# Projection tiles in pairs by seven block products in place of eight, in a five-branch mixer kernel

## The chip, the cores and the metric

The kernel runs on one core of one Trainium2 chip. The metric is the device time of one execution in microseconds (us). The core has five engines that run side by side, each working off its own list of instructions in order: PE (TensorE: matmuls), DVE (VectorE), ACT (ScalarE), POOL (GpSimd) and SP (SyncE, which here only issues DMA transfers). PEld is the loading of PE's stationary operand.

## The reference, cut to what matters

One layer of a decoder: 1024 tokens, width 1024, all in float32.

```
proj = h @ w_in + b_in                      # h: 1024 x 1024 (normed x), 94 used column tiles of 128
A    gated delta rule, 4 heads              # q, k, v: 12 tiles
B    GLU -> causal conv of width 31 -> LayerNorm -> swish      # 8 tiles
C    sliding-window attention, 8 heads over 2 kv heads         # cq 4, ck 1, cv 1
D    width-4 conv -> gated linear recurrence (a scan)          # dx 4
E    attention into 256 memory tokens, 4 heads                 # eq 4; w_mem_kv
ys[n]      = branch[n] * silu(z[n])                            # z: 5 x 4 tiles
merged     = sum_n sigmoid(gate[n]) * (ys[n] @ w_br[n])        # gate: 5 x 8 tiles
out        = x + rmsnorm(merged @ w_out)
```

So most of the matrix work is `h @ w_in`: 94 tiles, each 1024 (contraction) x 128 (columns) against 1024 tokens. Each branch product `ys[n] @ w_br[n]` contracts over 512.

## The kernel before

Float32 precision is had by splitting every operand into a high and a low part (`F32R` tiles): `mm3` issues three matmuls for one product of a 128 x 128 weight block with 128 x 512 tokens (high·high, high·low, low·high). The transposed, normed input is held for nearly the whole run as 8 tiles `hTh[k]` (high) and 8 tiles `hTl[k]` (low), 128 x 1024 each.

A projection tile is one *unit*: `wload` loads 512 KB of weights into `raw`, ACT copies it to `wh` (L222), POOL computes the rest `wl` (L223); `project` runs 2 token halves x 8 contraction steps x 3 = 48 matmuls into a PSUM tile `mm` of two banks (two such tiles take turns), and ACT or DVE evicts it. Eight contraction steps, k = 0 to 7, are two halves of four; the tokens are two halves `HL` and `HR` of 512. The list `units` sets the order: branch A's tiles, B's, the silu gates `az`, `eq`, then for each branch n `m_units(n)`: two gate tiles, then one branch unit `br` (48 matmuls from the branch's halves `yh`, `yl`, for two column tiles), and so on, four times; the gate (`sg`, L1004) multiplies the product on DVE (L1029) and POOL adds it to `merged` (L1032). `z_units` multiplies a finished branch by its silu (L972, POOL L955) and splits it into `yh`, `yl` (L958, L959).

The branches' own work runs in the *background*: generators (`gdn_all`, `conv_b`, `attn_e`, `lru`, `attn_c`) that are advanced by `tick()`, which `project` calls after every second contraction step, that is 8 times a tile. `start_bg` gives each a rate (steps per tick): conv_b 1.1, attn_e 1.0, lru 0.6, attn_c 1.0. `drain` runs a generator to its end at once. The program fixes dependences and priorities (`tc.high_priority` lifts an instruction above others); a scheduler turns them into one list per engine when the kernel is built, so at run time an engine that waits at the head of its list holds up everything behind it.

Names: `pc` is the convolution's accumulator in PSUM (L876, 120 steps on DVE), `u` its input, `rt`, `it`, `a2`, `th` belong to `lru`, `woh`/`wol` are the split `w_out`.

## Time and profile before

| | |
|---|---|
| time, median of 3 runs | 1665.55 us (1665.54 to 1666.98) |
| profiled execution: time / span of its instructions | 1666.35 us / 1664.6 us |
| PE, DVE, ACT, POOL busy share of the span | 97%, 51%, 39%, 36% |
| mean granted PE clock | 0.988 of full speed |
| DMA | 87.5 MB, mean 53 GB/s |

The span runs from the first to the last instruction of the profiled execution; its device time is 1.75 us longer. A busy share is an average over stages that are bound by different things. Matmuls overlap, so the sum of their durations is more than the time they take.

### The profile page before, as it was taken

Reading aid. Unit: us, or ns where it says so; the run is one execution under the profiler, and the core shown is the slowest. Engines: PE = TensorE matmul, PEld = TensorE weight load, DVE = VectorE, ACT = ScalarE, POOL = GpSimd, SP = SyncE. Lnnn points to the kernel's source line nnn. Section 1 sums busy time; section 2 is a strip of 40 time slices with the busy share of each in tenths; the row PEclk is TensorE's granted clock in tenths of the full one; section 3 lists DMA queues with packets and bytes.
Section 4 is the critical chain, followed back from the end, with each engine's and each line's share of the span. In section 5 each row is a group of like instructions: output and inputs, shape, how many; then the busy total and the mean of one; then the engine's idle time right before and its main releaser. Section 6 shows DMA issues by size and latency. Waiting matters only on the chain.

```text
span 1664.6 us, 19410 instructions
## 1 busy us (share of the span) xinstructions
PE 1613.9 (97%) x7846; PEld 1327.6 (80%) x7846; DVE 842.4 (51%) x1257; ACT 655.0 (39%) x1071; POOL 596.7 (36%) x315
## 2 busy tenths in 40 slices
PE   8989699999999998999999999999999999999998
PEld 7668588888888876888888877788888888888877
DVE  6678844376898886233564634211066664002712
ACT  6344123532421124435445276522266654212311
POOL 1354232422422237612345266554221222622021
PEclk9899899999999999999999999999999999999999
DMA  4112110110011110222011111112110101112322
GB/s 156 46 40 64 38 33 26 38 39 26 13 64 51 45 45 27 88 70 95 26 39 51 51 38 51 39 51 76 51 39 26 39 26 39 51 51 76 102 97 80
DMA packets 27129, 87.51 MB, mean 53 GB/s; under 512 B 5104, under 2 KB 6560, under 8 KB 26912
## 3 DMA queue, kind: packets, MB, share of 16 engines
q1 hardware_dynamic: 26896, 86.15, 15.9%
q8 instruction: 61, 1.00, 0.3%
q14 instruction: 28, 0.23, 0.0%
q10 hardware_dynamic: 144, 0.13, 0.0%
HBM read 82.06 MB, written 5.78 MB: 53 GB/s over the span
## 4 chain that ended last, share of the span: by engine, by line
PE 80%; DVE 14%; ACT 3%; POOL 2%; issue 1%; DMA 0%; DVEq 0%; ACTq 0%; POOLq 0%
PE mm L278 22%; PE mm L277 22%; PE mm L279 22%; DVE qk L484 2%; DVE lt L692 2%; DVE Ad L694 1%; PE pb L1451 1%; DVE v L484 1%; PE pb L722 1%; PE pa L722 1%; PE pa L1407 1%; DVE m L612 1%; PE pb L1439 1%; PE pa L664 1%; DVE p L1183 1%
## 5 line engine op out<-in xcount | busy, mean ns | idle before, releaser
L279 PE MATMUL mm<-hTh,wl 128*128 128x512 f32 x1472 | 591.4, 402 | 10.8 <-POOL wl L223 10.8
L277 PE MATMUL mm<-hTh,wh 128*128 128x512 f32 x1472 | 599.6, 407 | 0.0
L278 PE MATMUL mm<-hTl,wh 128*128 128x512 f32 x1472 | 594.1, 404 | 0.0
L223 POOL TENSOR_TENSOR wl<-raw,wh 128x1024 fp32r<-128x1024 f32 x113 | 276.4, 2446 | 638.5 <-ACT wh L222 638.1
L279 PEld LDWEIGHTS mm<-hTh,wl 128*128 128x128 f32 x1472 | 279.2, 190 | 69.6 <-POOL wl L223 11.9
L277 PEld LDWEIGHTS mm<-hTh,wh 128*128 128x128 f32 x1472 | 279.5, 190 | 58.7 <-issue 0.2
L278 PEld LDWEIGHTS mm<-hTl,wh 128*128 128x128 f32 x1472 | 279.5, 190 | 55.1 <-issue 3.1
L222 ACT ACTIVATE wh<-raw 128x1024 fp32r<-128x1024 f32 (+1 forms) x131 | 129.8, 998 | 387.1 <-issue 246.2
L876 DVE SCALAR_TENSOR_TENSOR pc<-u,sm,pc 128x1024 f32<-128x1024 f32 x120 | 154.7, 1289 | 3.8
L277 PE MATMUL mm<-yh,wh 128*128 128x512 f32 x320 | 127.8, 399 | 0.0
L278 PE MATMUL mm<-yl,wh 128*128 128x512 f32 x320 | 127.4, 398 | 0.0
L279 PE MATMUL mm<-yh,wl 128*128 128x512 f32 x320 | 126.8, 396 | 0.0
L972 DVE SCALAR_TENSOR_TENSOR sg<-mm,sm,sg 128x1024 f32<-128x1024 f32 x20 | 25.7, 1284 | 121.9 <-ACT sg L971 90.2
L1032 POOL TENSOR_TENSOR merged<-merged,sg 128x1024 f32<-128x1024 f32 x24 | 59.1, 2461 | 57.2 <-DVE sg L1029 35.9
L277 PEld LDWEIGHTS mm<-yh,wh 128*128 128x128 f32 x320 | 60.1, 188 | 13.0 <-DVE sgl L1029 0.2
L278 PEld LDWEIGHTS mm<-yl,wh 128*128 128x128 f32 x320 | 60.2, 188 | 12.5 <-issue 1.5
L279 PEld LDWEIGHTS mm<-yh,wl 128*128 128x128 f32 x320 | 60.1, 188 | 12.6
L1029 DVE TENSOR_TENSOR sg<-mm,sg 128x1024 f32<-128x1024 f32 x27 | 32.9, 1220 | 48.1 <-PE mm L279 30.3
L223 DVE TENSOR_TENSOR wol<-raw,woh 128x1024 fp32r<-128x1024 f32 x8 | 9.9, 1234 | 90.0 <-ACT woh L222 90.0
L1397 DVE TENSOR_TENSOR ql<-yC,qh 64x512 fp32r<-64x512 f32 x32 | 27.6, 863 | 54.1 <-ACT qh L1394 53.7
L1451 PEld LDWEIGHTS pb<-vt,pT 128*128 128x128 f32 x240 | 43.2, 190 | 9.2 <-ACT pT L1440 2.6
L1577 POOL TENSOR_TENSOR res<-res,xr 128x512 f32<-128x512 f32 x14 | 17.8, 1293 | 84.2 <-DVE res L1575 76.5
(428 smaller groups left out, 2441.3 us busy)
## 6 DMA issues: line engine op xcount, KB each, us to landing
raw<-in_w_t SPq DMA_DIRECT2D x94, 512.0 KB, 3.7
raw<-in_w_br SPq DMA_DIRECT2D x20, 512.0 KB, 3.6
xt<-in_x SPq DMA_DIRECT2D x8, 512.0 KB, 7.9
raw<-in_w_mem SPq DMA_DIRECT2D x8, 512.0 KB, 3.8
raw<-in_w_out SPq DMA_DIRECT2D x8, 512.0 KB, 3.8
xr<-in_x SPq DMA_DIRECT2D x8, 512.0 KB, 4.6
out_dram<-res SPq DMA_DIRECT2D x7, 512.0 KB, 2.9
d_rt<-d_rb SPq DMA_DIRECT2D x1, 1536.0 KB, 8.6
```

The source lines that it names most:

```text
L222: act.activation(hi, raw, AF.Copy)
L223: eng.tensor_tensor(out=lo, in0=raw, in1=f32(hi), op=ALU.subtract)
L277: pe.matmul(o, lh, rh, start=start, stop=False)
L278: pe.matmul(o, lh, rl, start=False, stop=False)
L279: pe.matmul(o, ll, rh, start=False, stop=stop)
L484: dve.scalar_tensor_tensor(out=acc, in0=xp[:, j:j + 1024], scalar=cw(j), in1=acc, op0=ALU.mult, op1=ALU.add)
L692: dve.tensor_tensor(out=t3, in0=V3[:, 0:r, j:j + 1].broadcast_to([P, r, n]), in1=A3[:, j:j + 1, j + 1:32].broadcast_to([P, r, n]), op=ALU. ...
L722: pe.matmul(ps[:, j * P:(j + 1) * P], lhs[:, j, :], rhs[:, j, :], start=True, stop=True)
L876: dve.scalar_tensor_tensor(out=acc, in0=u[:, j:j + 1024], scalar=w(j), in1=acc, op0=ALU.mult, op1=ALU.add)
L1029: dve.tensor_tensor(out=(merged[d] if first else sgs[d])[:, cl], in0=p2, in1=sgs[d][:, cl], op=ALU.mult)
L1032: (dve if last else pool).tensor_tensor(out=merged[d][:, cl], in0=merged[d][:, cl], in1=sgs[d][:, cl], op=ALU.add)
L1451: pe.matmul(po[:, i, g, :], pts[n, g][:, m, i * P:(i + 1) * P], vt[:, k0 // P + m, 64 * g:64 * g + 64], start=(m == 0), stop=(m == nk - 1))
```

## The change

Two 128-column tiles k0, k1 of `w_in` are taken as one 2 x 2 block product: the weights have blocks (tile k0 or k1) x (contraction half), the input has blocks (contraction half) x (token half). Seven products of sums of blocks, in place of eight products of blocks, give all four result blocks; each is 4 contraction steps x 3 = 12 matmuls of 512 tokens. The names in `prod(...)` are the input's block sums: `b11`, `b21`, `b22` are halves of `hTh`/`hTl`; `t1` to `t4` are differences, computed once by `blocks_h` (`t1` overwrites a quarter of `hTh`/`hTl` by `block_t1`). The sums of weight blocks are made per pair: four DVE additions (`preps`) and seven splits (`wblock`, ACT and POOL, 512 columns each). Products accumulate in PSUM banks X (two take turns), Y and Z (one each), and a bank is read by ACT (`keep`) or DVE (`plus`) between two products that accumulate in it.

The 20 tiles of A's q, k, v and B's inputs and 10 gate tiles stay as plain units. The other 64 tiles are 32 pairs. Their results, and the gated halves `yh`, `yl` of branches A, B, E and D, are stored to DRAM (`dram(key)`) and loaded again where they are used. All branch products come last (`run_branches`), with `attn_c` as background. Rates now: conv_b 1.1 (2.0 after the convolution), attn_e 1.1, lru 1.2, attn_c 1.0. The PSUM pool `mm` is closed while the pairs run.

```diff
-    def project(hi, lo):
+    def project(hi, lo, between=None):
...
+    def gated(n, zk, t, y, z_t):
+        while (zk, t) not in dr:
+            yield
+        zt, b = z_t(F32), bcol(zk, t)
+        sp.dma_start(zt, dr[zk, t])
+        yield from wait(3)
+        s = z_t(F32)
+        act.activation(s, zt, AF.Sigmoid, bias=b)
+        dve.scalar_tensor_tensor(out=zt, in0=zt, scalar=b, in1=s, op0=ALU.add, op1=ALU.mult)
+        pool.tensor_tensor(out=y, in0=y, in1=zt, op=ALU.mult)
+        yield from wait(2)
+        h, l = z_t(F32R), z_t(F32R)
+        act.activation(h, y, AF.Copy)
+        pool.tensor_tensor(out=l, in0=y, in1=f32(h), op=ALU.subtract)
+        sp.dma_start(dram(("yh", n, t)), f32(h))
+        sp.dma_start(dram(("yl", n, t)), f32(l))
+        yield from wait(2)
...
+    def wblock(x):
+        t = wp.tile([P, 2, 512], F32R, name=nm("wb"), tag=("raw", "wh", "wl")[wtag[0] % 3])
+        wtag[0] += 1
+        act.activation(t[:, 0, :], x, AF.Copy)
+        pool.tensor_tensor(out=t[:, 1, :], in0=x, in1=f32(t[:, 0, :]), op=ALU.subtract)
+        return t
...
+            def prod(o, hn, start):
+                w = blk()
+                for k in range(4):
+                    ks = slice(k * P, (k + 1) * P)
+                    mm3(o, w[:, 0, ks], w[:, 1, ks], *hb[hn, k], start and k == 0, k == 3, not start)
+                    if k % 2:
+                        tick()
+            u0, u1 = sg_t(), sg_t()
...
+            prod(X, "b11", True)
+            keep(u0[:, HL], X)
+            prod(Z, "t1", True)
+            keep(u1[:, HR], Z)
+            prod(X, "t2", False)
+            keep(u0[:, HR], X)
+            prod(Y, "b21", True)
+            plus(u0[:, HL], Y)
+            prod(X, "t3", False)
+            plus(u1[:, HR], X)
+            prod(Z, "b22", False)
+            plus(u0[:, HR], Z)
...
+            prod(X, "t4", False)
...
+            sp.dma_start(dram(k0), u0)
+            sp.dma_start(dram(k1), u1)
...
+        order = quad("az") + quad("bz") + quad("eq") + quad("ez") + quad("dx") + quad("dz")
+        tail = quad("cq") + [(("ck", 0), ("cv", 0))] + quad("cz")
+        pairs.extend(order + gp[:4] + tail + gp[4:])
...
+    def y_load(n):
+        for t in range(4):
+            for d, s in ((yh, "yh"), (yl, "yl")):
+                if n == 0:
+                    d[n, t] = pools["m"].tile([P, T], F32R, name=nm(s), tag=s, bufs=4)
+                else:
+                    d[n, t] = hp_.tile([P, T], F32R, name=nm(s), tag="hT")
+                sp.dma_start(f32(d[n, t]), dr[s, n, t])
...
+    def run_branches():
+        pools["pc"], st_["pc"] = open_pool("pc")
+        start("c", attn_c, 1.0)
+        order = [(n, dp) for n in (0, 1, 4, 3, 2) for dp in range(4)]
+        gl = [(n, 2 * dp + e) for n, dp in order for e in range(2)]
+        for g in gl[:3]:
+            gate_load(*g)
+        ng = 3
+        y_load(1)
+        w = wload(a["w_br"][0, 0], False)
```

**Where the rows move, PE.** Before, a tile's matmuls all use one weight tile (`wh`, `wl`) and the eight `hTh`, `hTl`; here the first six of 48.

```order
L277 MATMUL mm_3751<-hTh_101,wh_3682 128x512
L278 MATMUL mm_3751<-hTl_109,wh_3682 128x512
L279 MATMUL mm_3751<-hTh_101,wl_3683 128x512
L277 MATMUL mm_3751<-hTh_102,wh_3682 128x512
L278 MATMUL mm_3751<-hTl_110,wh_3682 128x512
L279 MATMUL mm_3751<-hTh_102,wl_3683 128x512
```

Now, the first product of the first pair (bank X, weight block `wb_3827`) and the first row of the next product (bank Z), from the same engine's list.

```order
L290 MATMUL X_3926<-hTh_102,wb_3827 128x512
L291 MATMUL X_3926<-hTl_110,wb_3827 128x512
L292 MATMUL X_3926<-hTh_102,wb_3827 128x512
L290 MATMUL X_3926<-hTh_103,wb_3827 128x512
L291 MATMUL X_3926<-hTl_111,wb_3827 128x512
L292 MATMUL X_3926<-hTh_103,wb_3827 128x512
L290 MATMUL X_3926<-hTh_104,wb_3827 128x512
L291 MATMUL X_3926<-hTl_112,wb_3827 128x512
L292 MATMUL X_3926<-hTh_104,wb_3827 128x512
L290 MATMUL Z_3927<-hTh_101,wb_3832 128x512
```

A product is 12 rows, a pair 84, and the whole list of PE has 384 matmuls fewer than before (32 x 12); everything else on PE is there in the same number.

**DVE while the convolution runs.** Before, between two gate multiplications (L1029) there are runs of convolution steps (L876).

```order
L1029 TENSOR_TENSOR merged_3948<-mm_3918,sg_3879 128x1024
L876 SCALAR_TENSOR_TENSOR pc_3647<-u_2109,sm,pc_3647 128x1024 x5
L873 TENSOR_SCALAR pc_3868<-u_2354,sm 128x1024
L876 SCALAR_TENSOR_TENSOR pc_3868<-u_2354,sm,pc_3868 128x1024 x12
L1029 TENSOR_TENSOR merged_4121<-mm_4087,sg_4014 128x1024
L876 SCALAR_TENSOR_TENSOR pc_3868<-u_2354,sm,pc_3868 128x1024 x3
L1029 TENSOR_TENSOR merged_4152<-mm_4123,sg_4079 128x1024
```

Now the same steps (L919) share the list with the weight sums (`rw`, L1141), the additions from the banks (`sg` from Y, X, Z, L1177) and branch A's silu (`zp`, L892); this is one pair's worth.

```order
L1141 TENSOR_TENSOR rw_4343<-rw_4192 128x512
L919 SCALAR_TENSOR_TENSOR pc_4186<-u_2109,sm,pc_4186 128x1024
L1141 TENSOR_TENSOR rw_4343<-rw_4343,rw_4190 128x512
L1141 TENSOR_TENSOR rw_4192<-rw_4190,rw_4192 128x512
L919 SCALAR_TENSOR_TENSOR pc_4186<-u_2109,sm,pc_4186 128x1024 x5
L1177 TENSOR_TENSOR sg_4250<-Y_4249,sg_4250 128x512
L919 SCALAR_TENSOR_TENSOR pc_4186<-u_2109,sm,pc_4186 128x1024
L892 SCALAR_TENSOR_TENSOR zp_4263<-zp_4263,sm,zp_4292 128x1024
L1177 TENSOR_TENSOR sg_4251<-X_4247,sg_4251 128x512
L1141 TENSOR_TENSOR rw_4190<-rw_4190,rw_4343 128x512
L919 SCALAR_TENSOR_TENSOR pc_4186<-u_2109,sm,pc_4186 128x1024
L1177 TENSOR_TENSOR sg_4250<-Z_4248,sg_4250 128x512
```

In the first eight pairs DVE's list holds 82 convolution steps, 4 silu steps, 2 first steps (L916) and 56 instructions of 512 columns.

**SP at the passage from the pairs to the branch products.** Before, SP's list is loads of weights one after the other.

```order
L229 DMA raw_9167<-in_w_t 128x1024
L229 DMA raw_9316<-in_w_br 128x1024
L229 DMA raw_9451<-in_w_t 128x1024
L229 DMA raw_9603<-in_w_t 128x1024
L229 DMA raw_9752<-in_w_br 128x1024
```

Now, at the last two pairs: `d_gt_4` and `d_gt_5` are the stores of the last pair but one, `it_8862` the load of D's last silu tile (`dz`, 3), `d_yh_3`, `d_yl_3` (of `it_8927` and `a_1247`) the stores of D's last gated halves, `yh_9...`/`yl_9...` loads of `y_load`.

```order
L1201 DMA d_gt_4_9460<-sg_9339 128x1024
L888 DMA it_8862<-d_dz_5860 128x1024
L1202 DMA d_gt_5_9462<-sg_9340 128x1024
L1714 DMA yh_9591<-d_yh_0_5419 128x1024
L1714 DMA yl_9593<-d_yl_0_5421 128x1024
L1731 DMA sg_9585<-d_gt_0_2830 128x1024
L898 DMA d_yh_3_8931<-it_8927 128x1024
L899 DMA d_yl_3_8933<-a_1247_8928 128x1024
L1714 DMA yh_9595<-d_yh_1_5455 128x1024
L1714 DMA yl_9597<-d_yl_1_5457 128x1024
L1714 DMA yh_9013<-d_yh_0_4142 128x1024
L1714 DMA yl_9015<-d_yl_0_4144 128x1024
```

Six more loads like the last two follow (yh_9017 to yl_9027), and then these rows, of which `raw_9607` is the weights of the first branch product.

```order
L1201 DMA d_gt_6_9573<-sg_9467 128x1024
L1202 DMA d_gt_7_9575<-sg_9468 128x1024
L1714 DMA yh_9599<-d_yh_2_5508 128x1024
L1731 DMA sg_9587<-d_gt_1_2923 128x1024
L1731 DMA sg_9589<-d_gt_2_3033 128x1024
L1714 DMA yl_9601<-d_yl_2_5510 128x1024
L1714 DMA yh_9603<-d_yh_3_5558 128x1024
L1714 DMA yl_9605<-d_yl_3_5560 128x1024
L241 DMA raw_9607<-in_w_br 128x1024
L241 DMA raw_9613<-in_w_br 128x1024
```

So from `yh_9595` to `raw_9607` there are 19 transfers of 512 KB, all behind the store of D's last gated half; `sg_9589` takes the buffer that `d_gt_7` is stored from.

## Rows read from the trace of the kernel before

**Rows 1.** The page's head: span, engines' busy time, granted clock by slice.

```profile
span 1664.6 us, 19410 instructions
PE 1613.9 (97%) x7846; PEld 1327.6 (80%) x7846; DVE 842.4 (51%) x1257; ACT 655.0 (39%) x1071; POOL 596.7 (36%) x315
PEclk9899899999999999999999999999999999999999
```

**Rows 2.** Timeline of PE, a stretch of gate tiles: start, duration, engine, line, operation.

```profile
1480.19 0.39 PE L277 MATMUL mm<-hTh,wh 128*128 128x512 f32 x1
...
1491.98 0.39 PE L278 MATMUL mm<-hTl,wh 128*128 128x512 f32 x1
```

**Rows 3.** Who waited for whom, PE: total us, times, longest.

```profile
PE mm L279 <- POOL wl L223: 10.8, 2, 5.9
PE pa L722 <- ACT gln L727: 8.4, 1, 8.4
```

**Rows 4.** Weight splits: by form, and by source (min/median/max ns).

```profile
L222 ACT ACTIVATE wh<-raw 128x512 fp32r<-128x512 f32 x18 | 10.4, 624 | 25.9 <-issue 8.7 <-DMA raw<-in_w_mem 8.2 <-PE mm L278 5.6
L223 POOL TENSOR_TENSOR wl<-raw,wh x113: 2341/2401/3407, 9.0 to 1548.6; 128x1024 fp32r<-128x1024 f32 x113
L223 DVE TENSOR_TENSOR wl<-raw,wh x18: 676/686/2901, 724.3 to 758.6; 128x512 fp32r<-128x512 f32 x18
L223 POOL TENSOR_TENSOR ql<-yE,qh x8: 1292/1298/1399, 763.9 to 850.0; 128x512 fp32r<-128x512 f32 x8
```

**Rows 5.** Evictions of 512 columns from PSUM, by source: ACT and DVE.

```profile
L1563 ACT ACTIVATE res<-mm x14: 598/598/600, 1578.7 to 1648.4; 128x512 f32<-128x512 f32 x14
L1198 DVE TENSOR_TENSOR pT<-pb,pT x16: 670/686/693, 779.9 to 892.3; 128x512 fp32r<-128x512 f32 x16
```

**Rows 6.** Timeline of DVE in the convolution.

```profile
520.83 1.35 DVE L873 TENSOR_SCALAR pc<-u,sm 128x1024 f32<-128x1024 f32 x1 [1.09 <-ACT accB L879]
522.21 15.87 DVE L876 SCALAR_TENSOR_TENSOR pc<-u,sm,pc 128x1024 f32<-128x1024 f32 x12
539.21 1.23 DVE L1029 TENSOR_TENSOR merged<-mm,sg 128x1024 f32<-128x1024 f32 x1 [1.14 <-PE mm L279]
```

**Rows 7.** Windows of 40 us: PE, PEld, DVE, ACT, POOL busy, PEclk, DMA.

```profile
520.00:560.00 40.00, 40.00 (x178) 33.13 (x177) 36.83 (x29) 8.06 (x8) 12.17 (x6) 1.00 0.13 41
640.00:680.00 40.00, 35.16 (x143) 28.56 (x143) 16.09 (x13) 13.23 (x15) 37.30 (x19) 0.91 0.15 53
```

**Rows 8.** Lines of `lru` on ACT, by form: busy, mean ns.

```profile
L1311 ACT ACTIVATE rt<-pa,sm 64x512 f32<-64x512 f32 x16 | 10.9, 684 | 26.2 <-PE pa L1310 26.1
L1319 ACT ACT_TABLE_LOAD x4 | 5.1, 1283 | 0.1
L1292 ACT ACTIVATE xs<-yD 64x1024 fp32r<-64x1024 f32 x8 | 8.4, 1054 | 8.0 <-DVE yD L1274 7.9
```

**Rows 9.** Silu and split of a gated branch, by form.

```profile
L971 ACT ACTIVATE sg<-mm,sm 128x1024 f32<-128x1024 f32 x20 | 22.1, 1104 | 2.2 <-POOL qk L955 2.1
L972 DVE SCALAR_TENSOR_TENSOR sg<-mm,sm,sg 128x1024 f32<-128x1024 f32 x20 | 25.7, 1284 | 121.9 <-ACT sg L971 90.2 <-POOL wl L223 21.9 <-POOL yl L959 9.8
L959 POOL TENSOR_TENSOR yl<-yD,yh 128x1024 fp32r<-128x1024 f32 x4 | 9.6, 2404 | 4.7 <-ACT yh L958 4.7
```

**Rows 10.** DMA: 512 KB, us to landing; a window of queued loads (share, GB/s).

```profile
raw<-in_w_t SPq DMA_DIRECT2D x94, 512.0 KB, 3.7
out_dram<-res SPq DMA_DIRECT2D x7, 512.0 KB, 2.9
2.00:14.00 12.00, 1.00 1.00 391
```

**Rows 11.** Windows of 4 us after a wait of PE in the LayerNorm.

```profile
660.00:664.00 4.00, 0.00 (x0) 0.00 (x0) 0.00 (x0) 1.06 (x1) 4.00 (x3) 0.95 0.00 0
664.00:668.00 4.00, 3.21 (x8) 2.57 (x9) 0.00 (x0) 0.00 (x0) 4.00 (x3) 0.50 0.38 131
668.00:672.00 4.00, 4.00 (x14) 3.21 (x13) 0.00 (x0) 2.57 (x3) 2.83 (x2) 0.69 0.00 0
```

More of the change, by code (lines that the diff above doesn't have):

```diff
@@ new lines, in gate_unit, with fn, plain_tasks @@
+    def gate_unit(key):
+        def fn(hi, lo, between=None):
+            ps = project(hi, lo, between)
+            sg = sg_t()
+            with tc.high_priority(offset=300):
+                act.activation(sg, ps.rearrange("p a b -> p (a b)"), AF.Sigmoid, bias=bcol(*key))
+            sp.dma_start(dram(key), sg)
+        return a["w_t"][_TIDX[key]], fn, pool
+    def plain_tasks():
+        yield from units
+        for i in range(40):
+            if i == 4:
+                yield None, lambda: drain("g"), None
+            if not ("g" in bgs or "ts" in bgs or len(gates) % 2):
+                return
+            yield gate_unit(gates.pop(0))
@@ L1158, in attn_e @@
         qs, pts, pp = {}, {}, {}
+        for h in range(4):
+            sp.dma_start(y[h], dr["eq", h])
+        yield from wait(3)
         def split(h, hf):
@@ L1188, in trans @@
             if tp == 0:
[L1189 removed]
+                pts[h, hf] = [pt_t(i, F32R, [P, 2, 512]) for i in range(2)]
             pt = pb_t()
@@ L1349, in trunk, with z_t, advance @@
-    ev(open_c)
-    def ck_fn(hi, lo):
-        ps = project(hi, lo).rearrange("p a b -> p (a b)")
+            yield from wait(3)
+        turn = [0]
+        def z_t(dt):
+            turn[0] += 1
+            return work(("a2", "it")[turn[0] % 2], dt)
+        for t in range(4):
+            yield from gated(3, "dz", t, yD[t], z_t)
+    stage = [0]
+    def advance():
+        if stage[0] == 0 and "cb" not in bgs and "fa" not in bgs:
+            open_e()
+            start("mem", mem_norm)
+            stage[0] = 1
+        elif stage[0] == 1 and "mem" not in bgs:
+            stage[0] = 2
+            return [mem_item(i) for i in range(8)]
+        elif stage[0] == 2 and "pe2" in pools and "e" not in bgs:
+            open_d()
+            start("d", lru, 1.2)
+            stage[0] = 3
+        elif stage[0] == 3 and "d" not in bgs:
+            st_["pd"].close()
+            pools["m"], st_["m"] = open_pool("m", side="right")
+            y_load(0)
+            stage[0] = 4
+        return []
@@ new lines, in trunk, with choose @@
+    items, queue, ready = [], [], []
+    nprep = [0, 0]
+    def choose():
+        queue.extend(advance())
+        while not queue and not pairs and stage[0] < 2:
+            for n in list(bgs):
+                drain(n)
+            queue.extend(advance())
+        it = queue.pop(0) if queue else (pair_item(*pairs.pop(0)) if pairs else None)
+        if it is not None:
+            with tc.high_priority(offset=2000):
+                it["begin"]()
+            items.append(it)
+        return it
@@ new lines, in prep, with stream_begin @@
+    def prep():
+        i, j = nprep
+        if i == len(items):
+            if choose() is None:
+                return False
+        it = items[i]
+        if j == 2 and i + 1 == len(items):
+            choose()
+        with tc.high_priority(offset=2000):
+            ready.append(wblock(it["preps"][j]()))
+        nprep[:] = (i, j + 1) if j + 1 < len(it["preps"]) else (i + 1, 0)
+        return True
+    def stream_begin():
+        make_pairs()
+        for _ in range(LEAD):
+            prep()
@@ new lines, in run_stream, with blk @@
+    def run_stream():
+        psl_close("m")
+        psl_open("x")
+        i = 0
+        def blk():
+            prep()
+            return ready.pop(0)
+        while True:
+            if i == len(items):
+                if nprep[0] == len(items) and not prep():
+                    break
+            items[i]["run"](blk)
+            i += 1
+        while stage[0] < 4:
+            for n in list(bgs):
+                drain(n)
+            assert not advance()
+        st_["hs"].close()
+        psl_close("x")
+        psl_open("m")
@@ L1531, in trunk @@
-    run_units()
-    for d in range(8):
-        dump(f"dbg_mg{d}", merged[d])
+                p2 = ps.rearrange("p a b -> p (a b)")[:, cl]
+                with tc.high_priority(offset=300):
+                    dve.tensor_tensor(out=(merged[d] if first else sg)[:, cl], in0=p2, in1=sg[:, cl], op=ALU.mult)
+                if not first:
+                    (dve if last else pool).tensor_tensor(out=merged[d][:, cl], in0=merged[d][:, cl],
+                                                          in1=sg[:, cl], op=ALU.add)
```

602 lines of the change are left out of this document (338 added, 264 removed).

## The prediction

> **What bounds the kernel now.** First the head of the page [rows 1]: TensorE (PE) is busy 97% of the span, the next engine 51%, and the granted clock is at its upper level in nearly every slice. So the time is PE's work, plus the little it waits. Then the price of one matmul. The 0.39 us that the timeline gives as its duration is not it, since matmuls overlap. From the start of the first to the start of the last of 53 rows without a gap are 11.79 us, so one costs 11.79 / 52 = 0.2267 us [rows 2]. Last the list of waits, for what PE loses: the two largest are 10.8 us for late weight splits and 8.4 us inside branch A [rows 3]. PE is idle 1664.6 - 1613.9 = 50.7 us in all, and a change that leaves the places alone leaves the waits.
>
> **What it removes.** 32 pairs lose 12 matmuls each: 384 x 0.2267 = **87.0 us**. The lists of the two programs show the same number, and no matmul is added.
>
> **What each pair must now fit into.** Per product PE needs 12 x 0.2267 = 2.72 us, per pair 84 x 0.2267 = 19.04 us (before 21.76). Against that stand, per pair:
> - POOL: seven splits of 512 columns at 1.30 us = 9.1 us (before two of 1024 at 2.40) [rows 4];
> - ACT: seven copies at 0.62, some six evictions at 0.60 and a sigmoid, together 8 to 9 us [rows 4, 5];
> - DVE: four weight sums and three additions from PSUM at 0.69 = 4.8 us [rows 4, 5].
> None of them alone reaches 19.04 us. What the background adds decides, and there are three places where it comes close.
>
> *The convolution (first eight pairs).* Twelve steps took 15.87 us back to back, 1.32 us each [rows 6]. DVE's list there holds 82 steps, 4 silu steps of the same form, 2 first steps of 1.36 and 56 instructions of 512 columns, at 0.69 and the 0.03 us between two: 86 x 1.32 + 2.7 + 56 x 0.72 = 156.5 us, against 8 x 19.04 = 152.3 us on PE. Before, DVE was at 37 of 40 us here and PE lost nothing [rows 7], but there a PSUM tile could wait a whole tile's 10.9 us for its eviction, and now X can wait one product, 2.72 us, before the next sum into it. So PE loses what DVE is over, less the slack: 0 to 12 us, I take **4**.
>
> *The LayerNorm and the gating of B (pairs 9 to 12).* Before, POOL was busy 37 of 40 us there and PE waited 4.8 us of its 40 [rows 7]. In the new lists POOL holds 74 us for these four pairs against 80 us of PE. The old loss stays; I add 0 to 12 us, and take **2**.
>
> *The recurrence (`lru`, pairs 24 to 28).* Its rate is doubled, 0.6 to 1.2. ACT's list holds 35 block copies (0.62), 32 gate activations (0.68), 14 table loads (1.28), 25 evictions and short sigmoids (0.60), 6 splits (1.05) and 24 others of 1024 columns (about 1.1) [rows 4, 5, 8, 9]: 21.7 + 21.9 + 18.0 + 15.0 + 6.3 + 26.4 = 109.3 us, against 101 us of PE (420 matmuls of 2.72 us a dozen, and the recurrence's own). Eight us over, of which the six weight blocks that can be split ahead (5 x 2.72 us of lead) take most: 0 to 15 us, I take **3**.
>
> At the start of the stream, `block_t1` (four copies and four subtractions, 8 x 0.65) lies under the last plain half tile of 5.4 us: 1 us at most, I take **1**.
>
> **The way by DRAM.** 74 tiles and 32 halves of 512 KB are stored and loaded again: 212 x 0.524 MB = 111 MB more, 199 MB in all. The DMA engines moved 391 GB/s where loads were queued [rows 10], so this is some 510 us of their 1600, and under the pairs it is hidden. It is not hidden at the passage to the branch products. Let T be the end of the last pair's last product.
> 1. The load of D's last silu tile stands on SP behind a store of the last pair but one, so it goes out about T - 20 and lands at T - 16 [rows 10].
> 2. Sigmoid 1.1, DVE 1.28, POOL 2.4, copy 1.06, POOL 2.4 [rows 9]: its last half is ready at about T - 8. Until then SP can't pass `d_yl_3`.
> 3. From there to the first branch weights are 19 transfers of 512 KB. At 391 GB/s each takes 1.34 us: 25.5 us, and about 2 us until the first moves (3.7 to landing less 1.34). So `raw_9607` lands at about T + 19.5.
> 4. ACT 1.06 and POOL 2.40 split it, while the first two matmuls (0.45) need only the high part: PE is held to about T + 22.5. I take **22 us**.
> The floor, if SP were free in time, is the forced chain: eviction 0.6, store of gate 7 landed 2.9, its buffer reloaded, four issues of 0.4, load 3.7, split 3.0, about 12 us. If D's tail is 15 us later than its list has it, 37 us. After a wait of 5.5 us in the LayerNorm the next 8 us ran at a mean clock of 0.6 [rows 11], a loss of 3.2 us; the same is due here: **3 us**. [...]
>
> The branch products themselves are 20 units of 48 matmuls, as before; weights, gates and halves are five transfers of 512 KB per unit of 10.9 us, 240 GB/s, below the 391, and each is asked for a unit ahead. No term.
>
> **Sum.** 1664.6 - 87.0 + 4 + 2 + 3 + 1 + 22 + 3 = 1612.6 us of span; 1.75 us lie outside, so 1614.4 for that execution, which was 0.8 above the median of the runs: **1613.5 us**.
>
> **Rivals.**
> - *No gap at the passage.* The first weights wait for no data, only for SP; if SP gets through in time, or the clock holds, 1613.5 - 25 = 1588 us. Against it: the list has nineteen transfers in front, and the floor is 12 us. Chance 0.13.
> - *The other engines set the pace.* If the static lists of DVE, ACT and POOL hold PE up by 2 us in each of the 17 pairs counted above, that is 34 in place of 9: 1639 us, and with a passage of 37 us 1653. For it: DVE and ACT are within 5% of PE, and an engine that waits at the head of its list holds up the copies behind. Chance 0.19.
> - *Slower: the evictions miss their 2.72 us.* In each pair seven products go into four banks, and the sums into X and Z wait for a copy or addition that may itself wait behind a convolution step (1.32 + 0.69 = 2.0 us, plus the signals). If every one of the 224 products waits 0.39 us, the 87 us are gone; with 0.6 us, 1613.5 + 134 - 9 = 1738 us. Against it: three of four evictions have no such step ahead. Chance 0.04.
> - *Slower: short waits at each bank change bring the clock down.* Over the 32 pairs, 609 us, a mean clock of 0.87 would cost 91 us and undo the gain: 1613.5 + 91 = 1704 us. In the rows the clock falls behind a wait of 5.5 us [rows 11], and a change of bank costs nothing where the eviction is in time. Chance 0.03. [...]
> - That the 384 matmuls aren't saved is excluded by PE's list.
>
> **How the numbers follow.** The forecast (a gap of 12 to 35 us, small losses in the pairs) holds 0.59, from 1598 to 1632 us; no gap 0.13; pace 0.19; slower 0.07; a mix that ends within 0.2% 0.02. A difference under 0.2% (3 us) can't be told from none for this kernel. Faster 0.59 + 0.13 + 0.19 = 0.91. The range reaches to the no-gap case and most of the pace case: 1587 to 1648 us.
>
> **What would show it.** Right: PE's busy time down by about 87 us; between the last X product and the first `yh` matmul one hole of 15 to 30 us that ends on the split of `raw`, SP in the stretch before it waiting on D's store; 4-us windows at half clock behind it; in the first eight pairs DVE over 95% and PE waits named after L1177. Wrong: no hole there; or waits of PE on `keep`, `plus` or `wblock` that sum to more than 40 us; or the granted clock below 0.95 through the pairs.

## The result, and the profile after

The changed kernel takes 1771.98 us (median of four runs, 1770.60 to 1772.91), the kernel before 1665.55 (four runs): ratio 1.0637, 95% interval 1.0618 to 1.0655. It is slower by 106 us where 52 us less was forecast.

The head of the page after, against [rows 1]:

```profile
span 1771.2 us, 20034 instructions
PE 1577.3 (89%) x7462; PEld 1277.8 (72%) x7462; DVE 1073.6 (61%) x1503; ACT 760.1 (43%) x1348; POOL 795.0 (45%) x492
PEclk9999899999999999887999999899996999999999
```

The 384 matmuls are gone (7846 to 7462). PE is idle 1771.2 - 1577.3 = 193.9 us, before 50.7: 143.2 us more. Its busy time fell by 36.6 us and not by 87.0, so what is left takes 50.4 us longer. Most of that is the clock, whose mean granted share fell from 0.988 to 0.948: 115.0 us of PE's busy time lie at the lower of its two levels (half clock: its records have 1.0 and 0.5 only), before 31.1, and half of the difference, 42.0 us, is my estimate of what it costs (behind the wait at 615.6 us a matmul starts every 0.43 us at half clock, ahead of it every 0.227). The three add up: -87.0 + 143.2 + 50.4 = 106.6 us, the difference of the two spans.

Where PE waits now, against [rows 3] (total us, times, longest; five of the larger rows):

```profile
PE X L290 <- ACT sg L1173: 66.8, 12, 30.8
PE mm L290 <- ACT wh L234: 24.3, 1, 24.3
PE X L290 <- DVE sg L1177: 14.2, 9, 3.3
PE pa L1452 <- DVE xs L1434: 10.4, 4, 4.4
PE Z L290 <- DVE sg L1177: 7.2, 4, 3.7
```

The second is the forecast hole at the passage. The first, third and last are products that wait until the partial sum in their bank has been read: `keep` (L1173) and `plus` (L1177). None of these existed before. The fourth is a product of the recurrence that waits for its split on DVE.

Five stretches of the same program (width, then busy us of PE, PEld, DVE, ACT, POOL, then PEclk, DMA share, GB/s): the convolution (two rows), branch B's gating, the recurrence, and the passage; against [rows 7].

```profile
520.00:560.00 40.00, 33.90 (x144) 27.32 (x143) 35.15 (x32) 14.74 (x23) 25.37 (x16) 0.95 0.45 158
640.00:680.00 40.00, 36.74 (x156) 29.91 (x155) 35.47 (x33) 12.78 (x22) 19.03 (x15) 0.96 0.38 132
760.00:800.00 40.00, 19.07 (x80) 15.00 (x79) 12.72 (x10) 10.78 (x14) 24.54 (x14) 0.80 0.42 149
1160.00:1200.00 40.00, 33.50 (x122) 24.80 (x121) 22.33 (x19) 31.73 (x41) 24.22 (x14) 0.87 0.33 116
1340.00:1360.00 20.00, 1.22 (x2) 0.50 (x2) 0.00 (x0) 2.11 (x2) 1.36 (x1) 0.50 0.96 349
```

From 760 to 800 us no engine is busy even two thirds of the time, and PE runs under half of it. That is not an engine that is full, it is a chain in which one waits for the next. The timeline of ACT there (start, duration, what it did, in brackets how long it stood idle before and for whom) is the view of this document to remember:

```profile
780.32 1.15 ACT L891 ACTIVATE zb<-zb,sm 128x1024 f32<-128x1024 f32 x1 [6.30 <-DMA zb<-d_bz]
781.38 0.61 ACT L1121 ACTIVATE wb<-rw 128x512 fp32r<-128x512 f32 x1
786.24 1.06 ACT L896 ACTIVATE zb<-u 128x1024 fp32r<-128x1024 f32 x1 [4.25 <-POOL u L893]
787.20 0.61 ACT L1121 ACTIVATE wb<-rw 128x512 fp32r<-128x512 f32 x1
794.22 1.15 ACT L891 ACTIVATE zb<-zb,sm 128x1024 f32<-128x1024 f32 x1 [6.40 <-DMA zb<-d_bz]
799.13 1.06 ACT L896 ACTIVATE zb<-u 128x1024 fp32r<-128x1024 f32 x1 [3.77 <-POOL u L893]
808.94 1.06 ACT L1235 ACTIVATE jk<-memx 128x1024 f32<-128x1024 f32 x1 [8.75 <-DMA memx<-in_mem]
...
810.00 0.58 ACT L1173 ACTIVATE sg<-X 128x512 f32<-128x512 f32 x1
810.47 0.59 ACT L1173 ACTIVATE sg<-Z 128x512 f32<-128x512 f32 x1
```

The two `keep` at 810 us read banks that PE had filled by about 771 and 774 us. They take 0.6 us each, and ACT was idle most of the time; but ahead of them in its list stand two tiles of gating (L891 waits for a load from DRAM, L896 for POOL's product) and the memory's norm, which waits for its own load. PE stands still for 30.8 us behind an engine that does nothing.

Why ACT's list is so late is seen on SP, which loads a tile of `z`, stores the gated halves and only then loads the next:

```profile
773.39 0.45 SPq L888 DMA_DIRECT2D zb<-d_bz  x1
...
789.74 0.32 SPq L899 DMA_DIRECT2D d_yl<-zb  x1
790.15 0.38 SPq L888 DMA_DIRECT2D zb<-d_bz  x1
```

One gated tile is a chain of 790.15 - 773.39 = 16.8 us: load, sigmoid on ACT, DVE, POOL, copy on ACT, POOL, store. The stores of the upper halves give the spacing of all 16 tiles, from the first to the last of four (A, B, E, D):

```profile
L898 SPq DMA_DIRECT2D d_yh<-zp x4: 319/319/320, 541.2 to 593.1; - x4
L898 SPq DMA_DIRECT2D d_yh<-zb x4: 319/320/382, 755.9 to 800.2; - x4
L898 SPq DMA_DIRECT2D d_yh<-pT x4: 319/320/320, 1049.5 to 1100.7; - x4
L898 SPq DMA_DIRECT2D d_yh<-it x4: 319/320/320, 1277.6 to 1323.8; - x4
```

A third of each is 17.3, 14.8, 17.1 and 15.4 us a tile. The program gives such a tile 7 steps, and PE takes 1.36 us for a step at rate 1 (half a product of 2.72): 9.5 us for A, 4.8 for B (rate 2.0), 8.7 for E (1.1), 7.9 for D (1.2). The chain is longer than the stretch of PE's list that it was laid beside, so what stands behind it in ACT's, DVE's and POOL's lists comes late, the evictions among it, and PE waits for them.

Over all 224 evictions (start of the eviction less the end of the last matmul into the bank, worked out from the trace) the median lateness of each kind is 0.4 to 1.6 us, within the 2.72 us that they have; 62 are over 2.3 us late, the worst 48 us. 40 of the 62 fall into the stretches in which a tile is being gated. PE's own waits for evictions in the rows above are 25, 88.2 us in all: the loss is a few long waits, not many short ones.

### The profile page after: what moved, and what is told of

Same layout as the page of the kernel before. It is cut to its first block, busy times and chain, and to the rows that moved or that the text cites. A ratio compares the mean times of both kernels' runs of the same rounds, so it can differ in the third digit from the quotient of the medians.

```text
span 1771.2 us, 20034 instructions
## 1 busy us (share of the span) xinstructions
PE 1577.3 (89%) x7462; PEld 1277.8 (72%) x7462; DVE 1073.6 (61%) x1503; ACT 760.1 (43%) x1348; POOL 795.0 (45%) x492
## 5 line engine op out<-in xcount | busy, mean ns | idle before, releaser
L1122 POOL TENSOR_TENSOR wb<-rw,wb 128x512 fp32r<-128x512 f32 x240 | 343.8, 1439 | 308.4 <-ACT wb L1121 293.3
L235 POOL TENSOR_TENSOR wl<-raw,wh 128x1024 fp32r<-128x1024 f32 x50 | 124.7, 2494 | 263.0 <-ACT wh L234 262.6
L1121 ACT ACTIVATE wb<-rw 128x512 fp32r<-128x512 f32 x240 | 149.9, 627 | 210.8 <-PE X L292 103.8
L292 PE MATMUL mm<-hTh,wl 128*128 128x512 f32 x448 | 184.9, 413 | 7.4 <-POOL wl L235 7.4
L290 PE MATMUL mm<-hTh,wh 128*128 128x512 f32 x448 | 188.8, 421 | 0.3 <-ACT sg L1057 0.3
L291 PE MATMUL mm<-hTl,wh 128*128 128x512 f32 x448 | 186.3, 416 | 0.0
L290 PE MATMUL mm<-yh,wh 128*128 128x512 f32 x320 | 139.6, 436 | 31.5 <-ACT wh L234 24.3
L919 DVE SCALAR_TENSOR_TENSOR pc<-u,sm,pc 128x1024 f32<-128x1024 f32 x120 | 154.0, 1284 | 2.1
L1141 DVE TENSOR_TENSOR rw<-rw,rw 128x512 f32<-128x512 f32 x96 | 99.2, 1059 | 56.1 <-POOL wb L1122 55.5
L290 PE MATMUL Z<-hTh,wb 128*128 128x512 f32 x256 | 104.7, 409 | 7.3 <-DVE sg L1177 7.2
L292 PEld LDWEIGHTS mm<-hTh,wl 128*128 128x128 f32 x448 | 85.8, 192 | 24.1 <-POOL wl L235 8.3
L292 PE MATMUL Z<-hTh,wb 128*128 128x512 f32 x256 | 102.6, 401 | 0.0
L290 PEld LDWEIGHTS mm<-hTh,wh 128*128 128x128 f32 x448 | 86.0, 192 | 16.8 <-ACT sg L1057 0.7
L291 PEld LDWEIGHTS mm<-hTl,wh 128*128 128x128 f32 x448 | 86.1, 192 | 13.6
```

Of the source, the lines that this page charges most:

```text
L235: eng.tensor_tensor(out=lo, in0=raw, in1=f32(hi), op=ALU.subtract)
L290: pe.matmul(o, lh, rh, start=start, stop=False, skip_group_check=again)
L291: pe.matmul(o, lh, rl, start=False, stop=False, skip_group_check=again)
L292: pe.matmul(o, ll, rh, start=False, stop=stop, skip_group_check=again)
L919: dve.scalar_tensor_tensor(out=acc, in0=u[:, j:j + 1024], scalar=w(j), in1=acc, op0=ALU.mult, op1=ALU.add)
L1121: act.activation(t[:, 0, :], x, AF.Copy)
```

## The experiments

All runs of a row were timed beside the kernel before on the same chip. "Stream" is the time from the first product of the pairs to the first branch product, from PE's timeline; PE idle is span less PE busy.

| kernel | us | ratio to before | PE busy | PE idle | stream |
|---|---|---|---|---|---|
| before | 1665.55 | 1 | 1613.9 | 50.7 | - |
| changed | 1771.98 | 1.0637 (1.0618 to 1.0655) | 1577.3 | 193.9 | 860 |
| eight products | 1738.43 | 1.0445 (1.0429 to 1.0461) | 1628.4 | 107.2 | 822 |
| evictions first | 1766.59 | 1.0615 (1.0595 to 1.0636) | 1573.4 | 195.0 | 857 |
| gating slower | 1764.55 | 1.0607 (1.0591 to 1.0622) | 1581.1 | 181.2 | 863 |
| branch weights first | 1771.77 | 1.0637 (1.0619 to 1.0655) | 1586.3 | 186.9 | 842 |
| thin convolution | 1748.08 | 1.0495 (1.0468 to 1.0522) | 1573.1 | 179.1 | 836 |
| copy on POOL | 1781.11 | 1.0693 (1.0674 to 1.0713) | 1578.8 | 199.2 | 866 |
| double slack | 1776.84 | 1.0665 (1.0649 to 1.0681) | 1583.1 | 190.9 | 864 |
| two thirds of PE | 1726.87 | 1.0370 (1.0354 to 1.0385) | 1395.4 | 331.1 | 828 |
| pairs alone | 1558.55 | 0.9363 (0.9347 to 0.9380) | 1487.6 | 69.4 | 640 |
| remedy | 1742.24 | 1.0465 (1.0450 to 1.0481) | 1578.2 | 161.9 | 814 |
| no gating | 1680.82 | 1.0095 (1.0078 to 1.0112) | 1555.9 | 124.0 | 762 |
| eight, gating spread | 1728.77 | 1.0379 (1.0364 to 1.0395) | 1634.0 | 90.1 | 806 |

Pair times below run from the start of the first matmul into Y of one pair to that of the next.

**Eight products.** The seven products are undone, and with them the weight sums, the additions and the short time that a bank has for its eviction; the stream, the route and the order of the branches stay.

```diff
-            prod(X, "b11", True)
-            keep(u0[:, HL], X)
...
-            prod(X, "t4", False)
+            for key, other in ((k0, "Z"), (k1, "Y")):
+                X, Z = bank("X", 2), bank(other, 1)
...
+                for e, hns in enumerate((("b11", "b12"), ("b21", "b22"))):
+                    w = blk()
+                    for o, hn, cl in zip((X, Z), hns, (HL, HR)):
```

> Eight block products per pair in place of seven, in the same stream, with the route by way of DRAM and the branch products last kept: no weight sums on DVE, no additions into kept banks, 4 weight blocks and 4 evictions per pair in place of 7 and 7, and a bank has four products (10.9 us) before it is written again in place of one (2.72 us). Late evictions (the theory): the 384 matmuls come back, 87 us, but the 110 to 140 us that PE lost inside the pairs go, so 1715 to 1750 us. The route and the order (rival): the loss has nothing to do with seven products and stays, so 1772 + 87 = 1859 us. Too much work on the engines beside PE (rival): DVE loses its sums and additions, which helps in the convolution's stage alone (25 us), so about 1830 us.

1738 us, as the theory had it. With 384 matmuls more it is 34 us faster. B's gated tiles are no quicker here (their stores are 14.3 us apart), but a bank has four products' time before it is written again, and PE's waits for the pairs' evictions come to 4.8 us. Many of its pairs take exactly 21.8 us, and what PE waits for in the stream is almost only the background's own matmuls (PE's waits of this kernel, the two longest there):

```profile
PE pa L1214 <- DVE memx L1207: 16.3, 1, 16.3
PE pa L1421 <- DVE xs L1403: 10.2, 3, 8.7
```

But it does the matmuls of the kernel before and is 73 us slower than that: the route and the order cost too, whatever the products.

**Evictions first.** `keep`, `plus` and the last eviction at priority 3000 in place of 300.

```diff
-                with tc.high_priority(offset=300):
+                with tc.high_priority(offset=3000):
                     act.activation(o, i, AF.Copy)
```

> The evictions of a pair's banks get a higher priority than the weight copies (3000 in place of 300), so that they stand ahead of the copies of the next blocks where both are ready; no work is added or left out. Late evictions behind ready copies: the copies make up 33 us of the time that late evictions waited on ACT, so 10 to 30 us less, 1742 to 1762 us. Late evictions behind instructions that themselves wait (for DMA, POOL or PE): the order among ready ones hardly matters, 1765 to 1775 us. Too much work on the engines, or the route: 1772 us.

Five us less. The order among ready instructions hardly matters; what stands ahead is not ready itself.

**Gating slower.** 12 steps a tile in place of 7, branch B's at 1.1 a tick.

```diff
-        yield from wait(3)
+        yield from wait(5)
...
-        yield from wait(2)
+        yield from wait(4)
...
-        yield from wait(2)
+        yield from wait(3)
...
+        bgs["cb"][1] = 1.1
```

> The gating of a branch tile is spread over more of PE's products (12 steps in place of 7, and branch B's at 1.1 steps in place of 2.0 for each half product); the same instructions, further apart in the lists. Late evictions (the theory): the 58 us pair and the waits behind the gating's activations shrink, 30 to 60 us less, 1712 to 1742 us, unless the background then runs past the last pair, which would show as a longer hole at the passage. Too much work on the engines, or contention: the work is the same, so 1772 us within 5.

The pair of 58.2 us fell to 30.7, and the pairs' last product came at 1293 us and not at 1334, as the theory wants: the instructions are the same, and only their places changed. Then the background was not done and ran on with no pairs beside it (PE's waits, this kernel):

```profile
PE pb L1590 <- ACT vr L1583: 34.5, 1, 34.5
```

What the pairs gained was paid back at the passage, and 7 us are left.

**Branch weights first.** The first branch weights are asked for ahead of the gates and of branch B's tiles.

```diff
+        w = wload(a["w_br"][0, 0], False)
         for g in gl[:3]:
             gate_load(*g)
         ng = 3
         y_load(1)
-        w = wload(a["w_br"][0, 0], False)
```

> At the passage from the pairs to the branch products the first branch weights are asked for ahead of the three gates and the eight tiles of branch B, not behind them; the same transfers. If the hole of 24 us is the place in SP's queue: about 15 us less, 1757 us, with a hole of about 9 us left (transfer, the copy on ACT, the split on POOL). If the hole is the transfers themselves, or SP's wait for the last pair's stores: 5 us or less, 1767 to 1772 us.

The first branch product starts 1.2 us after the last of the pairs, but the next wait for weights is that of the second (in PE's waits, against 24.3 us for the first):

```profile
PE mm L290 <- ACT wh L234: 9.1, 1, 9.1
```

The two windows behind the last pair:

```profile
1340.00:1360.00 20.00, 13.82 (x53) 9.07 (x51) 2.45 (x2) 0.98 (x2) 0.00 (x0) 0.99 0.96 361
1360.00:1380.00 20.00, 13.01 (x47) 10.05 (x48) 3.78 (x3) 9.35 (x10) 2.34 (x1) 0.66 0.93 355
```

The DMA engines are 96 and 93% busy here, and 96% in the changed kernel's row from 1340 us; the time is the same, as the rival had it. The rows fit a hole that is made by the transfers themselves: PE's idle time and half clock are spread over a longer stretch and not gone.

**Thin convolution.** DVE's time for the convolution goes, its place in the lists stays.

```diff
-                dve.scalar_tensor_tensor(out=acc, in0=u[:, j:j + 1024], scalar=w(j), in1=acc,
+                dve.scalar_tensor_tensor(out=acc[:, 0:64], in0=u[:, j:j + 64], scalar=w(j), in1=acc[:, 0:64],
```

> Each of the 120 convolution steps (1.28 us on DVE) works on 64 of its 1024 columns, which leaves out most of the convolution; every list has the same instructions in the same order but for this. DVE is then about a third busy in the first eight pairs. Late evictions because DVE is busy with convolution steps ahead of the additions (39 us of the lateness): the first eight pairs come to 19.0 to 19.5 us each in place of 22.2, so 20 to 25 us less, and 10 us of half clock less behind them, 1737 to 1750 us. Late evictions because the instruction ahead of them waits for ACT or POOL: the pairs stay above 21 us, 1760 to 1772 us.

24 us less. The fifth to seventh pair come to 19.0 us; the second to fourth, where branch A is gated, stay at 27.2, 20.3 and 23.3 (28.2, 20.8 and 23.4 in the changed kernel). So DVE's steps have a part in the later half of this stage, and gating costs the earlier half. In the later half it takes both: with the gating left out and the whole convolution there (below), the fifth to eighth pair come to 19.0, 19.0, 20.7 and 19.0 us. Of the 121 us taken off DVE (1073.6 to 953.0 us busy) a fifth shows in the time.

**Copy on POOL.** ACT's copy of the gated tile goes to POOL, so that ACT never waits for POOL's product.

```diff
-        act.activation(h, y, AF.Copy)
+        pool.tensor_copy(h, y)
```

> The upper half of each gated branch tile is rounded by POOL in place of ACT (16 copies of 128x1024), so that ACT's list, where the evictions stand, holds nothing any more that waits for POOL's product; POOL gets 16 more operations. Late evictions behind ACT's wait for POOL (38 us of the lateness): 20 to 40 us less, 1732 to 1752 us, with the 58 us pair at 40 us or less. POOL as the bound, or the wait moves to POOL's split of the weight blocks: no gain or a loss, 1765 to 1790 us.

Nine us slower. PE waits less for ACT's evictions and more for DVE's (its waits in this kernel):

```profile
PE X L290 <- ACT sg L1173: 43.9, 13, 23.7
PE Z L290 <- DVE sg L1177: 22.1, 8, 7.2
PE X L290 <- DVE sg L1177: 20.1, 10, 5.4
```

The wait does not belong to ACT's list. Taken from one list, it turns up in the next.

**Double slack.** The products in another order, `t4` of a pair after `t1` of the next, so that two products lie between a bank's eviction and its next writing.

```diff
-    LEAD = 4
+    LEAD = 3
...
             prod(Z, "t1", True)
             keep(u1[:, HR], Z)
+            late_run()
             prod(X, "t2", False)
...
-            prod(X, "t4", False)
+            w4 = blk()
+
+            def last():
+                prod(X, "t4", False, w4)
```

> The seven products of a pair in another order (b11, t1, the t4 of the pair before, t2, b21, b22, t3), so that at least two products, 5.44 us, lie between a bank's eviction and its next writing in place of one, 2.72 us; the weight blocks are prepared 3 ahead in place of 4; the same products, sums and evictions. Late evictions (the theory): of 62 evictions that start over 2.3 us late about 25 are over 5 us late, so about half of the gaps within the pairs go (132 us, the 31 us one stays) and half of the half clock, 50 to 80 us less, 1690 to 1725 us. The engines' work or the order in their lists sets the pace, however long a bank may wait: PE waits for its weight blocks in place of its banks, 1760 to 1775 us. One block less ahead matters: slower than 1775 us, with waits of PE on the split of the weight blocks.

Five us slower, and this was my theory's strongest forecast. Six of the first eight pairs do come to 19.0 or 19.2 us (windows of this kernel, the first two: PE 39.5 and 40.0 of 40 us). In the recurrence PE waits as before, at a lower clock (the last):

```profile
520.00:560.00 40.00, 39.54 (x174) 32.20 (x172) 36.93 (x37) 16.25 (x26) 25.62 (x17) 1.00 0.44 156
600.00:640.00 40.00, 40.00 (x176) 33.08 (x175) 39.07 (x38) 13.76 (x23) 21.17 (x17) 0.99 0.43 145
1160.00:1200.00 40.00, 35.03 (x117) 26.04 (x118) 19.77 (x16) 28.56 (x34) 19.76 (x13) 0.79 0.25 83
```

A second product of slack helps where an engine is merely busy. Where a chain of 15 us is laid beside 5 us of PE it does not: the pair of 58.2 us is 58.2 us again.

From here on the theory was another: the background's own chain, and not PE, sets the length of the stream.

**Two thirds of PE.** PE's part of the pairs is cut, and nothing else.

```diff
-                    mm3(o, w[:, 0, ks], w[:, 1, ks], *hb[hn, k], start and k == 0, k == 3, not start)
+                    pe.matmul(o, w[:, 0, ks], hb[hn, k][0], start=start and k == 0, stop=False, skip_group_check=not start)
+                    pe.matmul(o, w[:, 1, ks], hb[hn, k][0], start=False, stop=k == 3, skip_group_check=not start)
```

> The product of a weight block with the low half of the activations is left out of every block product of the pairs: two matmuls in place of three, 896 of 2688 x 3 / 9 = one third of the pairs' 2688 matmuls fewer, 203 us of TensorE at 0.2267 us; every eviction, weight block and step of the background stays. If PE with its waits sets the pace (late evictions, added to PE's own work): most of the 203 us comes off, 1570 to 1620 us. If the background's own chain and the lists that it shares with the evictions set the pace: the stream keeps some 800 us, less than 70 us comes off, above 1700 us, and TensorE stands idle for the rest.

203 us of matmuls less (32 pairs of 84, a third is 896), 45 us less time; the stream shrank from 860 to 828 us. The last pair ends 67 us earlier, but 61 us then pass before the first branch product, since the background is not done. PE is idle for 331.1 us, 77.1 of them in one wait for an eviction, and 32.9 in a matmul of the LayerNorm:

```profile
PE X L1165 <- ACT sg L1174: 96.2, 10, 77.1
PE pb L939 <- POOL lt L934: 32.9, 1, 32.9
```

The wait of 32.9 us ends behind the copy of the last convolution tile, the first of these rows of ACT. The wait of 77.1 us runs from 743 to 820 us; ahead of its eviction ACT has the rest of the LayerNorm, B's four tiles of gating (the second row is one of theirs) and the memory's norm:

```profile
725.70 1.02 ACT L922 ACTIVATE u<-pc 128x1024 f32<-128x1024 f32 x1 [29.80 <-DVE pc L919]
...
774.89 1.15 ACT L891 ACTIVATE zb<-zb,sm 128x1024 f32<-128x1024 f32 x1 [7.98 <-DMA zb<-d_bz]
```

In this window of the same kernel PE does nothing at all, and no other engine is busy half of the time:

```profile
760.00:800.00 40.00, 0.00 (x0) 0.00 (x0) 4.97 (x4) 5.46 (x5) 17.51 (x8) 0.50 0.45 163
```

**Pairs alone.** The background goes, with 248 matmuls of its own; of the edits, that of the gating:

```diff
     def gated(n, zk, t, y, z_t):
...
-        sp.dma_start(dram(("yh", n, t)), f32(h))
-        sp.dma_start(dram(("yl", n, t)), f32(l))
+        sp.dma_start(dram(("yh", n, t)), f32(hTh[t]))
+        sp.dma_start(dram(("yl", n, t)), f32(hTl[t]))
```

> The background of the pairs is left out (the convolution, LayerNorm, gating, the attention on memory, the recurrence; the branch tiles are stored from the input's halves in place of the gated results); the memory's norm and products, the pairs and all after them stay. If the pairs run freely by themselves: 19.0 to 19.3 us each, a granted clock of 1.00 through them, 835 us of the stream become about 650 (609 of pairs, the memory's products and its norm), 1572 to 1610 us. If the evictions are late by the weight copies and the sums alone, or the change of banks at every 2.72 us brings the clock down: pairs of over 20.5 us or a clock under 0.97 in them, above 1640 us.

Past the memory's products every pair takes 19.0 us, 84 x 0.2267, at full clock (two windows of this kernel):

```profile
840.00:880.00 40.00, 40.00 (x178) 33.15 (x177) 10.29 (x16) 13.44 (x24) 20.65 (x15) 1.00 0.34 108
1040.00:1080.00 40.00, 40.00 (x178) 33.15 (x177) 10.04 (x15) 17.66 (x28) 19.57 (x16) 1.00 0.31 105
```

The time lies 13 us under the range expected. So neither the weight sums, the splits nor the evictions are by themselves too slow for seven products, and no hole is left at the passage either (first branch product 2.1 us after the last of the pairs).

**Remedy.** Double slack, branch B's gating at 12 steps and 1.1 a tick, E's (and D's and A's) at 8, the attention at 1.6 steps to make room, branch weights first.

```diff
-        yield from wait(3)
+        yield from wait(5 if n == 1 else 3)
...
-        yield from wait(2)
+        yield from wait(4 if n == 1 else 3)
...
-        yield from wait(2)
+        yield from wait(3 if n == 1 else 2)
...
-                start("e", attn_e, 1.1)
+                start("e", attn_e, 1.6)
```

> The order with two products between a bank's eviction and its next writing, branch B's gating spread as before at 1.1 steps, branch E's by one step, the attention on memory at 1.6 steps in place of 1.1 to make room for it, and the first branch weights ahead of the gates and of branch B; the same work. If late evictions behind the gating are the cost: the 58 us pair falls under 32 us, the first eight pairs stay at about 20.5 us, 1700 to 1735 us. If the background's own chain sets the pace: what the pairs gain is lost at the passage, 1755 to 1780 us.

30 us less, a little above the first range. The longest wait of PE for an eviction is 6.2 us, but PE is idle 111 us more than in the kernel before (161.9 less 50.7), and its busy time is 51 us longer than the 1526.9 that the saving leaves (116.4 us of it lie at half clock, before 31.1); against that stand the 87 us saved.

**No gating.** The chain is cut at its front; the split and the stores stay.

```diff
-        zt, b = z_t(F32), bcol(zk, t)
-        sp.dma_start(zt, dr[zk, t])
-        yield from wait(3)
-        s = z_t(F32)
-        act.activation(s, zt, AF.Sigmoid, bias=b)
-        dve.scalar_tensor_tensor(out=zt, in0=zt, scalar=b, in1=s, op0=ALU.add, op1=ALU.mult)
-        pool.tensor_tensor(out=y, in0=y, in1=zt, op=ALU.mult)
-        yield from wait(2)
+        yield from wait(5)
```

> The gating of 16 branch tiles is left out (their load from DRAM, the sigmoid on ACT, the multiplication on DVE, the product on POOL); the two halves of the ungated tile are still made on ACT and POOL and stored, at the same steps. No matmul is left out. If the gating's chain through ACT, DVE and POOL, in the lists of the evictions, is the largest cost: the second to fourth pair, branch B's pairs and about half of the loss behind branches E and D come back, 80 to 110 us less, 1660 to 1692 us. If the background as a whole sets the pace and gating is but a part of it: 30 to 60 us less, 1712 to 1742 us. If the gating is hidden: 1760 to 1772 us.

91 us less: the largest single cost, and the whole slowdown but 15 us. What it left out is 16 loads and 16 times 1.15 us of ACT, 1.28 of DVE and 2.4 of POOL, which no engine lacked; what it took away is the chain. In PE's waits the evictions of the pairs come to 31 us, in place of 88; the two largest rows:

```profile
PE X L290 <- DVE sg L1170: 20.0, 6, 7.3
PE X L290 <- ACT sg L1166: 7.4, 5, 4.2
```

Two windows of this kernel, branch B's and the recurrence's:

```profile
760.00:800.00 40.00, 40.00 (x185) 32.77 (x184) 15.91 (x32) 21.81 (x45) 18.32 (x14) 1.00 0.33 119
1120.00:1160.00 40.00, 35.67 (x138) 26.77 (x137) 23.07 (x19) 31.36 (x39) 26.32 (x15) 0.91 0.28 92
```

The stretch from 760 to 800 us is whole again, the recurrence's is not: its loss is its own. And the passage has no hole, since the background is done before the pairs are. Of the 91 us, 38 are the pair of 58.2 us (now 20.0), 15 the first eight pairs (177.5 to 162.3 us), and 23 the hole at the passage (24.3 to 1.7 us). That POOL's products no longer run beside DVE's weight sums is a small part at most: the sums take 124.6 us of DVE in all, against 135.8.

**Eight, gating spread.** The first of these kernels with branch B's gating at 12 steps and 1.1 a tick, the others at 8 (the waits as in the remedy).

```diff
+        bgs["cb"][1] = 1.1
         for t in range(4):
             yield from gated(1, "bz", t, yB[t],
```

> Eight block products in place of seven as in the first of these kernels, and branch B's gating spread (12 steps at 1.1 in place of 7 at 2.0), branch E's and D's and A's by one step. The same work as in that one (1738 us). If the route by way of DRAM costs by where its gating stands: the wait of 16.3 us on the memory's norm goes and with it some 15 us at half clock, 1710 to 1725 us. If the route and the order cost it anyhow: 1735 to 1745 us.

Ten us less than eight products alone, less than expected. The wait on the memory's norm is gone (the longest in the stream is now 6.5 us, on `xs`); 63 us above the kernel before are left, 39 of them idle time of PE (90.1 less 50.7).

## Why the prediction was wrong

**Removed matmuls: right.** 384 fewer, 87 us of PE; on their own, with no background, the pairs run at the forecast 19.04 us.

**The step that failed** is the sentence on the way by DRAM, "under the pairs it is hidden". It was argued from bandwidth, and the transfers are hidden. But a load from DRAM in the background is also the first link of a chain through ACT, DVE and POOL, and its instructions stand in the same lists as the evictions. I worked that chain out once, for D's last tile at the passage, and gave the other 15 no price. It could have been had from [rows 8 to 10]: 3.7 + 1.1 + 1.28 + 2.4 + 1.06 + 2.4 = 11.9 us with no wait at all, against 9.5, 4.8, 8.7 and 7.9 us of PE: 4 x (2.4 + 7.1 + 3.2 + 4.0) = 67 us by this estimate. With the measured spacings (the load alone took 6.9 us from its issue to the sigmoid in the rows of B, not 3.7) it is 4 x (7.8 + 10.0 + 8.4 + 7.5) = 135 us. Neither is the loss itself, which also hangs on how long PE can do without the evictions: leaving the gating out gave back 91 us, and 23 of these are the hole at the passage, which the forecast had. With eight products, no hole and 4.8 us of waits for evictions, the route and the order together still cost 73 us.

**"None of them alone reaches 19.04 us"** and the three tight places were sums of busy time, engine by engine. They were the wrong measure: sums can't show a chain. The first eight pairs lost 25.2 us (177.5 less 152.3), where I took 4; branch B's stage includes one pair of 58 us, where I took 2 in all; pairs 24 to 28, with the recurrence, take 23 to 30 us each, 134 in all against the 101 of PE, where I took 3 over.

**The passage: right in place and size, wrong in worth.** The hole was 24.3 us for the forecast 22, behind D's last gated half and the loads, at half clock (0.50 in the row from 1340). But asking for the weights first gained nothing, and where the background ended sooner (eight products, no gating) there was no hole.

**The clock: right in kind, wrong in size.** I took 3 us behind one wait; 27 stretches at half clock, 186 us in all against 40 before (worked out from the clock's records; it agrees with 2 x (1 - 0.948) of the span), cost by that estimate some 42 of the 50 us that PE's busy time is longer, behind many waits and not one. (The wait of [rows 11] that I read as 5.5 us is 4.8 us: 660 to 664 and 0.79 of the next row. The 3 us do not hang on it.)

**The rivals.** "The other engines set the pace" named the right mechanism, lists that hold each other up, and sized it at 2 us for each of 17 pairs; PE stood idle 143 us more than before, 24 of them at the passage. "The evictions miss their 2.72 us" had the sign, but meant 0.6 us at every product behind a convolution step; it is 62 evictions of 224, 40 of them while a tile is being gated. "Short waits at each bank change bring the clock down": alone, the pairs change banks every 2.72 us at a clock of 1.00, so the change by itself does not. There are no waits at the changes there; where waits of some us came, in the changed kernel, the clock did fall (to half speed for 3.4 us at one of 2.6 us, for 6.8 us at one of 6.1 us). My own list of signs said it: waits on `keep` and `plus` over 40 us (88), and the clock under 0.95 through the pairs (0.935 from the first to the last).

**What is shown and what is not.** Shown: the pairs by themselves run freely; a third less PE work in them gives back 45 of 203 us; the gating costs 91 us, the hole at the passage included, though no engine lacks the time for it; seven products cost 34 us more than eight in this stream, though they have 87 us less of matmuls. Only argued: how the rest divides, the recurrence's own chain and DVE's convolution steps above all; and which of the things that eight products undo at once (the short time of a bank, the sums, the additions, three of seven splits) gives back how much. A version of the stream in which the gating of two tiles overlaps was not tried, since the buffers are one tile deep, and none of these kernels beats the one before with its work complete.

## What to carry to other kernels

Before you price background work by the sum of an engine's busy time, walk its chain once, load to store, and set it against the stretch of the main engine's list that it is laid beside; if the chain is longer, whoever stands behind it in those lists comes late, and the main engine pays as soon as it needs one of them. Making the main engine's work shorter shortens exactly that stretch. An eviction that a matmul waits for should share its list only with instructions whose inputs are surely there. Here a second product of slack, a higher priority or another engine for the waiting copy gained nothing or 5 us; the stream of eight products, with four products' time for an eviction, lost 4.8 us to them.

## What the hardware showed that was not expected

The weight sums on DVE (two SBUF operands, 128x512) took 0.69 us in the 64 cases in which no POOL operation ran beside them and 1.44 us on average in the other 64, up to 2.88:

```profile
L1141 DVE TENSOR_TENSOR rw<-rw,rw x96: 677/692/2876, 433.8 to 1307.7; 128x512 f32<-128x512 f32 x96
```

I had priced all of them at 0.69; why the other 64 took longer no run here shows.

In the changed kernel the clock fell at waits that look harmless. In the windows below PE stood still for 2.6 us from 615.6 us on, and the clock's records have it at half speed for 3.4 us from 617.8 us on; in the kernel before, six stretches at half speed made 40 us in all.

```profile
611.00:615.00 4.00, 4.00 (x20) 3.30 (x19) 3.93 (x5) 0.63 (x1) 2.52 (x2) 1.00 0.00 0
615.00:619.00 4.00, 1.38 (x5) 0.86 (x4) 3.96 (x6) 0.63 (x1) 1.27 (x1) 0.85 0.00 0
619.00:623.00 4.00, 4.00 (x14) 3.19 (x14) 3.96 (x4) 0.37 (x1) 0.00 (x0) 0.73 0.73 251
```
